# Attention scores of two heads at a time on the two 64-row halves of the TensorE array

## The chip, the cores and the metric

The kernel runs on one core of a Trainium2 chip. The time is device microseconds (us) of one execution. A profiled execution also leaves a trace with the start, the length and the waits of each instruction on each engine: PE is TensorE's matrix products, PEld its loads of stationary weights, DVE VectorE, ACT ScalarE, POOL GpSimd, SP the engine that issues most weight transfers.

## The reference

Two transformer layers on one sequence of 512 tokens and 1024 channels, in float32, each with adaptive norms (`ada_w` times an activated vector gives shifts, scales and gates), an attention and a mixture of 32 experts.

```python
def diff_attention(h, ...):                 # layer 0: 8 heads, two maps (cc) of 64 channels each
    q, k, v = split(h @ w_in, 3)            # rotary on the first 16 of each 64 channels
    s = einsum('cbhqd,cbhkd->cbhqk', qb, k) * d ** -0.5      # d = 64, causal
    a = softmax(s[0]) - lam_full * softmax(s[1])
    o = rmsnorm(a @ v) ...
def nsa_attention(h, ...):                  # layer 1: 16 heads of 64 channels, 2 kv groups
    s_c = qb . k_cmp     # 31 compressed blocks; p_c @ v_cmp
    s_s = qb . k_sel     # all 8 blocks are selected: plain causal attention, own k and v
    s_w = qb . k_win     # window of 512: plain causal attention, own k and v
    o = g0 * o_c + g1 * o_s + g2 * o_w
x = x + g1 * attention(...);  x = x + g2 * hier_moe(...)
```

## The kernel before

Products that need more than one fast pass are split by hand: a float32 tensor is written as a high part in `F32R` (a float32 type that one pass of the array takes) and the rest, a low part, and three products (high.high, high.low, low.high) are added up in PSUM. `dense` does this for the projections: for each of 8 chunks of the contraction it makes `wh` (ACT, L346) and `wl` (DVE, L347) and runs three products for each of four token tiles (L350 to L352).

A head has 64 channels and the array has 128 rows, and the kernel fills the other 64 rows with the split. The query and key rows that come out of a projection are copied twice side by side (`twice`, `dup_in`: L492, L493 in layer 0, L1044 in layer 1), rotated by `rope` on POOL (four instructions, L305 to L308), and transposed 128 columns at a time (L500, L1051), so that each head's 64 channels stand in rows 0 to 63 and again in rows 64 to 127. `stack_q` (L362 on ACT, L363 on DVE) then makes one tile with the high part of q in rows 0 to 63 and the low part in rows 64 to 127. `stack_k` (L358, L359) makes two tiles of k, high and low, each of them in both halves. In `scores`, one product of the stacked q with high k gives high.high plus low.high (L367), one with low k gives the rest (L369), and between them an identity in bf16 adds the causal mask to the last 128 columns (L368). The result of one head for 128 queries and n keys (n is 128, 256, 384 or 512, for query tile i = 0 to 3) fills n columns of one PSUM bank.

`softmax_rows` takes the row maximum on DVE (L374) and the exponential with its sum on ACT (L375) from that bank. There are eight banks, in three kinds: "mm" (4, also the accumulators of `dense` and of the adaptive norms, L189), "sc" (2) and "tr" (2, for transposes). Layer 0 takes its scores in "sc" alone; layer 1 takes "sc" twice and "mm" three times in every five heads.

The work of layer 0 is written out in an order (`v0 h0 q1 a8 h1 h2 ...`: v and q units are projections, h are heads, a are steps of the adaptive norms); `diff_rows` (one head, one query tile: two `scores`, softmaxes, difference, transposes L535, product with v L540) has a higher priority than what is around it, and a scheduler at build time places each engine's instructions by its own simulation. Layer 1 runs `nsa_block(gi, i)` for two kv groups and four query tiles: for "s" and "w", eight heads of scores in two batches of four, a scaling (L1189), then for each key tile eight transposes (L1197), two copies (L1199) and two products with v (L1202). The compressed scores are done in the "w" half: 16 products of 32 columns (L1149, L1150) in one bank.

The experts follow each attention: 16 pairs of experts a layer, whose two halves stand in columns 0 to 63 and 64 to 127 of the array (`pair`, L852). Their weights are 100.7 MB a layer, fetched by SP into tiles (`slot0` to `slot7`, `ring`) that the attention uses too, as these come free.

## Time and profile before

| | |
|---|---|
| median of 3 runs | 1419.81 us (1417.21 to 1421.36) |
| the profiled execution | 1417.2 us, its span in the trace 1415.4 us |
| mean granted TensorE clock | 0.957 of full speed |
| PE busy | 1289.2 us, 91% of the span |
| DVE, ACT, POOL busy | 787.2, 513.0, 188.4 us |

The span goes from the first to the last instruction; 1.8 us of the execution lie around it. Matrix products overlap in the array, and the trace models their ends, so a length of 0.40 us does not say that the array was taken for so long: the time from one start to the next says that, and it is what is read below. Layer 0's projections and heads stand at about 60 to 320 us, its experts at about 390 to 660, layer 1's projections at 700 to 815, its attention blocks at 815 to 1045, its experts from about 1130 on.

### The profile page before, as it was taken

The page shows a single profiled execution, that of the slowest core. Times are in us where ns is not written, and L with a number is a line of the kernel's source. Part 1 is how long each engine was busy: PE and PEld are TensorE (multiplying, and loading weights), DVE is VectorE, ACT ScalarE, POOL GpSimd, SP SyncE. Part 2 cuts the span into 40 slices and gives each one's busy share as a digit, 9 for nine tenths or more (in the row PEclk, how much of TensorE's full clock was granted, in tenths as well). Part 3 has the DMA queues.
Part 4 walks back from the last instruction along what each step waited for, and adds up shares of the span by engine and source line. Part 5 has one row for each costly group of instructions (what it writes and reads, how often), then busy time and mean ns, then how long its engine had stood idle before and what let it go on. Part 6 is the DMA issues. An engine that isn't in the chain of part 4 may idle for free.

```text
span 1415.4 us, 18254 instructions
## 1 busy us (share of the span) xinstructions
PE 1289.2 (91%) x6431; PEld 760.4 (54%) x6431; DVE 787.2 (56%) x1791; ACT 513.0 (36%) x1188; POOL 188.4 (13%) x298
## 2 busy tenths in 40 slices
PE   4899999978879999999799799999999599999995
PEld 0687658567733544444588465556558434444342
DVE  2444756486535666655653365657635445666555
ACT  2453544454322222111453345555644222222212
POOL 0022020211110000000042211112120200000000
PEclk7999999989979999999899999999999799999998
DMA  8633673585569999992132474520063599999931
GB/s 265 218 92 129 226 236 122 185 280 194 181 240 362 389 408 407 380 346 95 52 110 90 126 251 138 139 70 1 30 183 119 167 363 376 401 409 408 363 144 60
DMA packets 104494, 309.82 MB, mean 219 GB/s; under 512 B 13776, under 2 KB 27568, under 8 KB 104388
## 3 DMA queue, kind: packets, MB, share of 16 engines
q1 hardware_dynamic: 93920, 288.59, 57.4%
q0 software_dynamic: 6240, 12.95, 2.7%
q10 hardware_dynamic: 4228, 6.96, 1.6%
q8 instruction: 55, 0.90, 0.3%
q14 instruction: 51, 0.42, 0.1%
HBM read 310.51 MB, written 6.33 MB: 224 GB/s over the span
## 4 chain that ended last, share of the span: by engine, by line
PE 65%; DVE 6%; DMA 3%; ACT 2%; issue 1%; POOL 1%; DVEq 0%; POOLq 0%; ACTq 0%
PE b_mm L852 17%; PE b_mm L1202 5%; PE b_sc L875 4%; PE b_mm L875 4%; PE b_tr L1197 3%; PE b_sc L886 2%; PE b_tr L840 2%; PE b_mm L886 2%; DVE xs L888 2%; PE b_mm L350 2%; PE b_mm L572 2%; PE b_mm L573 2%; PE b_mm L351 2%; PE b_mm L352 2%; PE b_mm L574 2%; PE b_sc L887 2%
## 5 line engine op out<-in xcount | busy, mean ns | idle before, releaser
L852 PE MATMUL b_mm<-slot,xT 128*64 128x512 f32 x640 | 200.0, 607 | 0.0
L852 PE MATMUL b_mm<-ring,xT 128*64 128x512 f32 x384 | 135.9, 597 | 0.0
L350 PE MATMUL b_mm<-wh,h_hi 128*128 128x512 f32 (+1 forms) x320 | 116.6, 394 | 8.3 <-ACT wh L346 6.6
L351 PE MATMUL b_mm<-wl,h_hi 128*128 128x512 f32 (+1 forms) x320 | 122.1, 390 | 0.0
L352 PE MATMUL b_mm<-wh,h_lo 128*128 128x512 f32 (+1 forms) x320 | 119.9, 386 | 0.0
L845 ACT ACTIVATE xT<-b_tr,col_sh,col_A 128x128 f32<-128x128 f32 x128 | 56.4, 454 | 148.2 <-DVE xT L847 146.9
L852 PEld LDWEIGHTS b_mm<-slot,xT 128*64 128x64 f32 x640 | 58.3, 139 | 87.7 <-issue 81.7
L888 DVE TENSOR_TENSOR xs<-xs,b_sc 128x512 f32<-128x512 f32 x128 | 83.1, 680 | 23.1 <-PE b_sc L887 23.1
L888 DVE TENSOR_TENSOR xs<-xs,b_mm 128x512 f32<-128x512 f32 x128 | 81.9, 679 | 19.3 <-PE b_mm L887 19.3
L826 POOL DMA_INDIRECT xg<-xr_d,toks x32 | 32.1, 1003 | 434.1 <-PE b_tr L840 417.5
L189 PE MATMUL b_mm<-ring,csil 128*32 128x512 f32 x384 | 79.2, 645 | 10.5 <-DMA ring<-in_ada_w_dram 5.6
L855 ACT ACTIVATE sl<-b_mm 128x256 f32<-128x256 f32 x32 | 12.3, 384 | 187.7 <-PE b_mm L852 187.7
L857 DVE TENSOR_TENSOR ac<-b_mm,sl 128x256 f32<-128x256 f32 x32 | 19.8, 618 | 108.4 <-ACT sl L855 108.4
L347 DVE TENSOR_TENSOR wl<-ring,wh 128x512 fp32r<-128x512 f32 (+1 forms) x80 | 53.6, 679 | 38.3 <-ACT wh L346 37.6
L374 DVE TENSOR_REDUCE nm<-b_sc 128x1 f32<-128x128 f32 (+3 forms) x116 | 54.4, 482 | 32.2 <-PE b_sc L369 31.2
L350 PEld LDWEIGHTS b_mm<-wh,h_hi 128*128 128x128 f32 x320 | 60.5, 192 | 20.1 <-ACT wh L346 7.5
L1199 ACT ACTIVATE pT<-b_tr 128x512 f32<-128x512 f32 x80 | 47.3, 597 | 62.6 <-PE b_tr L1197 62.2
L358 ACT ACTIVATE yh<-y 128x512 fp32r<-128x512 f32 x64 | 39.9, 632 | 79.4 <-DVE y L878 79.4
L352 PEld LDWEIGHTS b_mm<-wh,h_lo 128*128 128x128 f32 x320 | 60.7, 190 | 11.0
L351 PEld LDWEIGHTS b_mm<-wl,h_hi 128*128 128x128 f32 x320 | 60.6, 190 | 10.9
L852 PEld LDWEIGHTS b_mm<-ring,xT 128*64 128x64 f32 x384 | 39.9, 137 | 49.4 <-issue 46.7
L346 ACT ACTIVATE wh<-ring 128x512 fp32r<-128x512 f32 (+1 forms) x80 | 48.4, 614 | 46.3 <-PE b_mm L352 38.0
(327 smaller groups left out, 2683.5 us busy)
## 6 DMA issues: line engine op xcount, KB each, us to landing
ring<-in_ada_w_dram SPq DMA_DIRECT2D x96, 512.0 KB
slot<-in_moe_w_gate_dram SPq DMA_DIRECT2D x80, 512.0 KB
slot<-in_moe_w_up_dram SPq DMA_DIRECT2D x80, 512.0 KB
dn<-in_moe_w_down_dram SPq DMA_DIRECT2D x80, 512.0 KB
slot<-in_moe_w_down_dram SPq DMA_DIRECT2D x48, 512.0 KB
ring<-in_moe_w_gate_dram SPq DMA_DIRECT2D x48, 512.0 KB
ring<-in_moe_w_up_dram SPq DMA_DIRECT2D x48, 512.0 KB
ring<-in_diff_w_in_dram SPq DMA_DIRECT2D x24, 512.0 KB
```

The costliest lines, as they stand in the source:

```text
L189: mm(acc[32 * g:32 * g + 32, :], lhsT, w[:, c0:c0 + 512], start=(k == 0), stop=(k == KC - 1), skip_group_check=True)
L347: nc.vector.tensor_tensor(wl[:, :n], w[:, k, :], wh[:, :n].bitcast(F32), op=OP.subtract)
L350: mm(accs[t][:, :n], hi[:, k, tt], wh[:, :n], start=(k == 0), stop=False)
L351: mm(accs[t][:, :n], hi[:, k, tt], wl[:, :n], start=False, stop=False)
L352: mm(accs[t][:, :n], lo[:, k, tt], wh[:, :n], start=False, stop=(k == KC - 1))
L374: nc.vector.tensor_reduce(nm, b[:, :n], axis=AX.X, op=OP.max, negate=True)
L845: nc.scalar.activation(xT[:, k, :], src, AF.Identity, scale=g.Ac[:, k:k + 1], bias=g.shc[:, k:k + 1])
L852: mm(hb[64 * a:64 * a + 64, :].rearrange("p (z n) -> p z n", z=2), xT[:, k, 64 * a:64 * a + 64], gu(a, k), start=(k == 0), stop=(k == KC - ...
L875: mm(yb[64 * a:64 * a + 64, :], aT[:, k, 64 * a:64 * a + 64], dn(a, k, z), start=(k == 0), stop=(k == 1), skip_group_check=True)
L886: mm(b, st[:, t * P:(t + 1) * P], yh[:, zz], start=True, stop=False)
L888: nc.vector.tensor_tensor(g.xs[:, t, zz], g.xs[:, t, zz], b, op=OP.add)
L1202: mm(ob[64 * st:64 * st + 64, :], vst[nm][:, j, 64 * gi:64 * gi + 64], pTs[st], start=(nm == "s" and j == 0), stop=False, skip_group_check ...
```

## The change

Heads 2s and 2s+1 now stand side by side: rows 0 to 63 of a tile hold the 64 channels of the one, rows 64 to 127 those of the other, without any copy. So `rope` takes 8 blocks of 64 and not 16, a token tile needs four transposes and not eight, and one `stack_k` over q and k together (layer 0) or over q (layer 1) takes the place of two calls. `scores` takes two heads and two banks: each product exists twice, once on rows 0 to 63 and once on rows 64 to 127, written alternately, and the three parts high.high, high.low and low.high are now three products of 64 rows a head. The mask, whose contraction runs over 128 positions, is added in two halves of 64 a head (`id2`, `mask2`). In layer 0 both maps of a head are one such pair, with both "sc" banks; in layer 1 the two heads of a pair share k, whose tiles already hold it in both halves. The compressed scores become 24 products on 64 rows, in two banks, with two additions of the mask.

```diff
--- before.py
+++ after.py
@@ -141,10 +141,16 @@
     nc.gpsimd.iota(jp, pattern=[[1, P]], base=0, channel_multiplier=-1, allow_small_or_imprecise_dtypes=True)
     ident = cst.tile([P, P], F32, name="ident")
     nc.vector.tensor_scalar(ident, jp, 0.0, None, op0=OP.is_equal)
-    ident_b = cst.tile([P, P], BF16, name="ident_b")
-    nc.vector.tensor_scalar(ident_b, jp, 0.0, None, op0=OP.is_equal)
-    maskneg = cst.tile([P, P], BF16, name="maskneg")
-    nc.vector.tensor_scalar(maskneg, jp, 0.0, NEG, op0=OP.is_gt, op1=OP.mult)
+
+    j2 = ring[1][:, P:2 * P]
+    for a in range(2):
+        nc.gpsimd.iota(j2[64 * a:64 * a + 64], pattern=[[1, P]], base=0, channel_multiplier=-1,
+                       allow_small_or_imprecise_dtypes=True)
+    id2 = cst.tile([P, 2, P], BF16, name="id2")
+    mask2 = cst.tile([P, 2, P], BF16, name="mask2")
+    for z in range(2):
+        nc.vector.tensor_scalar(id2[:, z], j2, 64.0 * z, None, op0=OP.is_equal)
+        nc.vector.tensor_scalar(mask2[:, z], j2, 64.0 * z, NEG, op0=OP.is_gt, op1=OP.mult)
     upper = cst.tile([P, P], BF16, name="upper")
     nc.vector.tensor_scalar(upper, jp, 0.0, None, op0=OP.is_gt)
     ones_b = cst.tile([P, P], BF16, name="ones_b")
@@ -358,16 +364,20 @@
         nc.scalar.activation(h_out, src, AF.Copy)
         nc.vector.tensor_tensor(l_out, src, h_out.bitcast(F32), op=OP.subtract)
 
-    def stack_q(src, dst):
-        nc.scalar.activation(dst, src, AF.Copy)
-        nc.vector.tensor_tensor(dst[64:128], src[64:128], dst[64:128].bitcast(F32), op=OP.subtract)
-
-    def scores(q, kh, kl, n, i, tag="sc"):
-        b = bank(tag)
-        mm(b[:, :n], q, kh, start=True, stop=False)
-        mm(b[:, i * P:n], ident_b, maskneg, start=False, stop=False, skip_group_check=True)
-        mm(b[:, :n], q, kl, start=False, stop=True)
-        return b
+    def scores(qh, ql, kh, kl, n, i, tags):
+
+        bs = [bank(tag) for tag in tags]
+        rows = [slice(0, 64), slice(64, 128)]
+        for a, b in enumerate(bs):
+            mm(b[:, :n], qh[rows[a]], kh[rows[a]], start=True, stop=False)
+        for z in range(2):
+            for a, b in enumerate(bs):
+                mm(b[:, i * P:n], id2[rows[a], z], mask2[rows[a], z], start=False, stop=False, skip_group_check=True)
+        for a, b in enumerate(bs):
+            mm(b[:, :n], qh[rows[a]], kl[rows[a]], start=False, stop=False)
+        for a, b in enumerate(bs):
+            mm(b[:, :n], ql[rows[a]], kh[rows[a]], start=False, stop=True)
+        return bs
 
     def softmax_rows(b, n, p_out, l_out):
         nm = sm.tile([P, 1], F32, name="nm")
@@ -484,26 +494,20 @@
         w = unit().rearrange("p (k n) -> p k n", k=KC)
         wload(w[:, :, 0:256], w_in[:, :, u * 256:(u + 1) * 256])
         wload(w[:, :, 256:512], w_in[:, :, D + u * 256:D + (u + 1) * 256])
-        qs, kh, kl = (slot(2 * i + u % 2, [P, 4, S], F32R) for i in range(3))
-        ST[u] = (qs, kh, kl)
+        qkh, qkl = (slot(2 * i + u % 2, [P, 4, S], F32R) for i in range(2))
+        ST[u] = (qkh, qkl)
 
         def evac(t, acc):
-            tmp = m.tile([P, 16, 64], F32, name="qkt", bufs=2)
-            nc.scalar.activation(twice(tmp[:, 0:8, :]), dup_in(acc[:, 0:256], 64), AF.Copy, scale=0.125)
-            nc.scalar.activation(twice(tmp[:, 8:16, :]), dup_in(acc[:, 256:512], 64), AF.Copy)
-            rope(m, tmp, t, 16)
+            tmp = m.tile([P, 8, 64], F32, name="qkt", bufs=2)
+            nc.scalar.activation(tmp[:, 0:4, :], acc[:, 0:256].rearrange("p (s d) -> p s d", d=64), AF.Copy, scale=0.125)
+            nc.scalar.activation(tmp[:, 4:8, :], acc[:, 256:512].rearrange("p (s d) -> p s d", d=64), AF.Copy)
+            rope(m, tmp, t, 8)
+            b = bank("tr")
+            for s in range(4):
+                nc.tensor.transpose(b[:, s * P:(s + 1) * P], tmp[:, 2 * s:2 * s + 2, :].rearrange("p a d -> p (a d)"),
+                                    ident)
             tt = slice(t * P, (t + 1) * P)
-            for half in range(2):
-                b = bank("tr")
-                for s in range(4):
-                    c0 = 2 * (half * 4 + s)
-                    nc.tensor.transpose(b[:, s * P:(s + 1) * P], tmp[:, c0:c0 + 2, :].rearrange("p a d -> p (a d)"),
-                                        ident)
-                bv = b.rearrange("p (s t) -> p s t", s=4)
-                if half == 0:
-                    stack_q(bv, qs[:, :, tt])
-                else:
-                    stack_k(bv, kh[:, :, tt], kl[:, :, tt])
+            stack_k(b.rearrange("p (s t) -> p s t", s=4), qkh[:, :, tt], qkl[:, :, tt])
 
         dense(qp, w, 512, hi, lo, evac, before)
 
@@ -515,14 +519,14 @@
         V[u] = v
         dense(qp, w, 512, hi, lo, lambda t, acc: copy_any(v[:, t, :], acc))
 
-    def diff_rows(h, i, qs, kh, kl, v, hc):
+    def diff_rows(h, i, qkh, qkl, v, hc):
         n = (i + 1) * P
         es = m.tile([P, 2, 512], F32, name="es", bufs=2)
         l2 = sm.tile([P, 2], F32, name="l2")
+        s = h % 2
+        bs = scores(qkh[:, s, i * P:n], qkl[:, s, i * P:n], qkh[:, 2 + s, :n], qkl[:, 2 + s, :n], n, i, ("sc", "sc"))
         for cc in range(2):
-            s = 2 * (h % 2) + cc
-            b = scores(qs[:, s, i * P:n], kh[:, s, :n], kl[:, s, :n], n, i)
-            softmax_rows(b, n, es[:, cc, :n], l2[:, cc:cc + 1])
+            softmax_rows(bs[cc], n, es[:, cc, :n], l2[:, cc:cc + 1])
 
         r = sm.tile([P, 2], F32, name="r2")
         nc.vector.tensor_scalar(l2, l2, 1e-30, None, op0=OP.max)
@@ -543,12 +547,12 @@
         nc.vector.tensor_scalar(o_n[:, i, h * P:(h + 1) * P], ob[:, 0:P], r[:, 0:1], None, op0=OP.mult)
 
     def diff_head(h):
-        qs, kh, kl = ST[h // 2]
+        qkh, qkl = ST[h // 2]
         v = V[h // 4]
         hc = slice((h % 4) * P, (h % 4 + 1) * P)
         for i in range(NT):
             with tc.high_priority(offset=0):
-                diff_rows(h, i, qs, kh, kl, v, hc)
+                diff_rows(h, i, qkh, qkl, v, hc)
         r = rsqrt_cols(oss[:, h, :], NT, 1.0 / P)
         for i in range(NT):
             oo = o_n[:, i, h * P:(h + 1) * P]
@@ -1041,16 +1045,14 @@
 
         def evac(t, acc):
             tmp = tp.tile([P, 16, 64], F32, name="qkt", bufs=4)
-            nc.scalar.activation(twice(tmp), dup_in(acc, 64), AF.Copy, scale=0.125)
-            rope(m, tmp, t, 16)
+            q8 = tmp[:, 0:8, :]
+            nc.scalar.activation(q8, acc.rearrange("p (s d) -> p s d", d=64), AF.Copy, scale=0.125)
+            rope(m, q8, t, 8)
             tt = slice(t * P, (t + 1) * P)
-            for half in range(2):
-                b = bank("tr")
-                for s in range(4):
-                    c0 = 2 * (half * 4 + s)
-                    nc.tensor.transpose(b[:, s * P:(s + 1) * P], tmp[:, c0:c0 + 2, :].rearrange("p a d -> p (a d)"),
-                                        ident)
-                stack_q(b.rearrange("p (s t) -> p s t", s=4), qs[half][:, :, tt])
+            b = bank("tr")
+            for s in range(4):
+                nc.tensor.transpose(b[:, s * P:(s + 1) * P], q8[:, 2 * s:2 * s + 2, :].rearrange("p a d -> p (a d)"), ident)
+            stack_k(b.rearrange("p (s t) -> p s t", s=4), qs[0][:, :, tt], qs[1][:, :, tt])
 
         dense(qp, w, 512, hi, lo, evac)
 
@@ -1144,12 +1146,18 @@
         for zi, nm in ((1, "s"), (2, "w")):
             if nm == "w":
 
-                b = bank("sc")
-                for h in range(8):
-                    mm(b[:, 32 * h:32 * h + 32], qs[h // 4][:, h % 4, tt], kch[:, 32 * gi:32 * gi + 32], start=True, stop=False)
-                    mm(b[:, 32 * h:32 * h + 32], qs[h // 4][:, h % 4, tt], kcl[:, 32 * gi:32 * gi + 32], start=False, stop=True)
+                bs = [bank("sc") for _ in range(2)]
+                rows = [slice(0, 64), slice(64, 128)]
+                gg = slice(32 * gi, 32 * gi + 32)
+                for s in range(4):
+                    for x, (qq, kk) in enumerate(((0, kch), (0, kcl), (1, kch))):
+                        for a in range(2):
+                            mm(bs[a][:, 32 * s:32 * s + 32], qs[qq][rows[a], s, tt], kk[rows[a], gg], start=(x == 0),
+                               stop=(x == 2))
                 sc = m.tile([P, 8, 32], F32, name="scm", bufs=2)
-                nc.vector.tensor_tensor(sc, b[:, 0:256].rearrange("p (h n) -> p h n", h=8), dup(mcmp[:, i, :], 8), op=OP.add)
+                for a in range(2):
+                    nc.vector.tensor_tensor(sc[:, a:8:2, :], bs[a][:, 0:P].rearrange("p (h n) -> p h n", h=4),
+                                            dup(mcmp[:, i, :], 4), op=OP.add)
                 mx = sm.tile([P, 8], F32, name="cmx")
                 nc.vector.tensor_reduce(mx, sc, axis=AX.X, op=OP.max)
                 nc.vector.tensor_tensor(sc, sc, mx[:, :, None].to_broadcast([P, 8, 32]), op=OP.subtract)
@@ -1174,12 +1182,15 @@
                     Pt = (m if pt[0] % 4 == 2 else m1).tile([P, 4, S], F32, name="Pt", tag="P", bufs=1)
                 Ps.append(Pt)
                 l4 = sm.tile([P, 4], F32, name="l4")
-                for hh in range(4):
-                    h = 4 * st + hh
-                    bb = scores(qs[h // 4][:, h % 4, tt], kst[nm][gi][0][:, 0:n], kst[nm][gi][1][:, 0:n], n, i,
-                                "mm" if sct[0] % 5 > 1 else "sc")
-                    sct[0] += 1
-                    softmax_rows(bb, n, Pt[:, hh, 0:n], l4[:, hh:hh + 1])
+                for s in range(2 * st, 2 * st + 2):
+                    tags = []
+                    for _ in range(2):
+                        tags.append("mm" if sct[0] % 5 > 1 else "sc")
+                        sct[0] += 1
+                    bs = scores(qs[0][:, s, tt], qs[1][:, s, tt], kst[nm][gi][0][:, 0:n], kst[nm][gi][1][:, 0:n], n, i, tags)
+                    for a in range(2):
+                        hh = 2 * (s % 2) + a
+                        softmax_rows(bs[a], n, Pt[:, hh, 0:n], l4[:, hh:hh + 1])
                 r = sm.tile([P, 4], F32, name="r4")
                 nc.vector.tensor_scalar(r, l4, 1e-30, None, op0=OP.max)
                 nc.vector.reciprocal(r, r)
```

## Rows read from the trace of the kernel before

**Rows 1.** The page: engines; the chain that ended last, by engine.

```profile
PE 1289.2 (91%) x6431; PEld 760.4 (54%) x6431; DVE 787.2 (56%) x1791; ACT 513.0 (36%) x1188; POOL 188.4 (13%) x298
...
PE 65%; DVE 6%; DMA 3%; ACT 2%; issue 1%; POOL 1%; DVEq 0%; POOLq 0%; ACTq 0%
```

**Rows 2.** Busy us (x instructions) in four stretches, granted clock, DMA.

```profile
60.00:280.00 220.00, 216.99 (x1157) 155.16 (x1156) 119.40 (x278) 101.11 (x257) 42.48 (x69) 1.00 0.50 161
280.00:320.00 40.00, 31.52 (x173) 24.32 (x172) 31.97 (x98) 22.19 (x75) 4.41 (x5) 0.87 0.88 283
...
780.00:815.00 35.00, 24.31 (x126) 15.86 (x126) 13.73 (x27) 10.60 (x19) 10.34 (x16) 0.93 0.42 128
815.00:1045.00 230.00, 228.77 (x1251) 124.97 (x1252) 135.79 (x405) 124.61 (x353) 38.43 (x32) 0.99 0.35 109
```

**Rows 3.** PE in time order: heads of 512 columns; start, length.

```profile
1001.93 0.40 PE L367 MATMUL b_mm<-slot,slot 128*128 128x512 f32 x1
1002.18 0.23 PE L368 MATMUL b_mm<-maskneg,ident_b 128*128 128x128 bf16 x1
1002.22 0.47 PE L369 MATMUL b_mm<-slot,slot 128*128 128x512 f32 x1
1002.53 0.40 PE L367 MATMUL b_mm<-slot,slot 128*128 128x512 f32 x1
...
1002.81 0.47 PE L369 MATMUL b_mm<-slot,slot 128*128 128x512 f32 x1
1003.21 1.07 PE L1202 MATMUL b_mm<-pT,v_w 128*64 128x512 f32 x2
```

**Rows 4.** PE in time order: heads of 128 and of 256 columns.

```profile
950.18 0.27 PE L367 MATMUL b_mm<-slot,slot 128*128 128x128 f32 x1
...
950.48 0.27 PE L367 MATMUL b_mm<-slot,slot 128*128 128x128 f32 x1
...
952.40 0.28 PE L367 MATMUL b_mm<-slot,slot 128*128 128x256 f32 x1
...
952.76 0.28 PE L367 MATMUL b_mm<-slot,slot 128*128 128x256 f32 x1
```

**Rows 5.** PE in time order: heads of 384 columns.

```profile
971.57 0.34 PE L367 MATMUL b_mm<-slot,slot 128*128 128x384 f32 x1
...
972.05 0.34 PE L367 MATMUL b_mm<-slot,slot 128*128 128x384 f32 x1
```

**Rows 6.** PE in time order: two products of a projection, 512 columns.

```profile
222.53 0.39 PE L350 MATMUL b_mm<-wh,h_hi 128*128 128x512 f32 x1
222.76 0.39 PE L351 MATMUL b_mm<-wl,h_hi 128*128 128x512 f32 x1
```

**Rows 7.** PE in time order: first and last of 16 compressed scores.

```profile
1004.21 0.28 PE L1149 MATMUL b_sc<-kch,slot 128*128 128x32 f32 x1
...
1005.91 0.26 PE L1150 MATMUL b_sc<-kcl,slot 128*128 128x32 f32 x1
```

**Rows 8.** Weight loads in time order: start of an expert pair.

```profile
423.96 0.13 PEld L852 LDWEIGHTS b_mm<-slot,xT 128*64 128x64 f32 x1 [0.25 <-issue]
423.96 0.13 PEld L852 LDWEIGHTS b_mm<-ring,xT 128*64 128x64 f32 x1
424.01 0.14 PEld L852 LDWEIGHTS b_mm<-slot,xT 128*64 128x64 f32 x1
```

**Rows 9.** PE in time order: an expert pair, and what follows.

```profile
549.24 6.60 PE L852 MATMUL b_mm<-ring,xT 128*64 128x512 f32 x29
555.77 0.51 PE L886 MATMUL b_sc<-yh,st 128*128 128x512 f32 x1
```

**Rows 10.** PE in time order: transposes of one token tile.

```profile
780.51 1.03 PE L1051 MATMUL b_tr<-ident,qkt 128*128 128x128 f32 x8
```

**Rows 11.** Groups by line: transposes, row maximum.

```profile
L500 PE MATMUL b_tr<-ident,qkt 128*128 128x128 f32 x128 | 19.3, 280 | 1.1 <-DVE slot L363 1.1
...
L374 DVE TENSOR_REDUCE nm<-b_sc 128x1 f32<-128x512 f32 x28 | 18.8, 685 | 8.2 <-PE b_sc L369 8.1
```

## The prediction

> **What bounds the kernel now.** I read the page first, then the busy time by stretches, then PE in order of time. The page says that PE is busy for 91% of the span and that 65% of the chain that ended last runs through it, DVE next with 6% [rows 1]. The stretches say where that matters for this change. From 60 to 280 us (projections and heads 0 to 5 of layer 0) PE is busy 217 of 220 us, from 815 to 1045 us (the blocks of layer 1) 228.8 of 230, at a granted clock of 1.00 and 0.99 of full speed, while DVE, ACT and DMA are near half or under [rows 2]. There a microsecond less on PE should be a microsecond less of time. Two stretches are otherwise: 280 to 320 us, where the last heads have little beside them (PE 31.5 of 40, DVE 32.0), and 780 to 815 us, the end of layer 1's projections (PE 24.3 of 35) [rows 2]. The experts take what comes before them as a starting line: their weights are loaded into tiles that the attention has to leave, so that an earlier end of the attention moves them forward whole.
>
> What a head costs on PE is read from start to start. Four heads of 512 columns in a row: high product to mask 0.25, mask to low product 0.04, low product to the next head 0.31 us; 0.60 in all [rows 3]. With 384 columns a head takes 0.48, with 256 0.36, with 128 0.30 [rows 4, 5]. There are 192 heads, 48 of each size: 48 x 1.74 = 83.5 us of PE when nothing stands between them, and somewhat more as they lie, since a run of heads that ends on a product of another shape costs 0.40 at its end and not 0.31 (low product at 1002.81, L1202 at 1003.21) [rows 3].
>
> **What two halves of the array do together.** No product of before uses 64 rows, so this is the price that the trace does not hold. The nearest rows are products on 64 columns. One alone (L1202, two passes) takes from 1003.21 to 1004.21, 0.50 a pass [rows 3, 7]. An expert pair alternates between the two column halves, and 29 passes of the same length take 6.53 us, 0.225 each [rows 9]: two halves run side by side. Their weight loads too: the first loads of the two halves start within 0.01 us of each other, and the second load of the first half follows 0.05 later [rows 8], so that each half has a queue of its own. I take the same for row halves: the two heads of a pair cost what one costs. The bounds are that, and no overlap at all.
>
> The Trainium skill ("TensorE: Matmul & The Clock Gate", Part 3, Measured speedup vs the span model) gives 3.07 for four row tiles of 32 at 512 columns; as an estimate from that figure, three quarters of full overlap would put the pairs at 2.53 + 0.63 = 3.16, and the scores' term at -7.7 in place of -22.8. No run here shows it yet.
>
> **The change part by part.** *Scores.* A head on its half now has high product, two masks, low product and a third product. That is the old head plus one mask (0.04) plus one product. A product with its load hidden costs 0.23 at 512 columns [rows 6], and I take three quarters of that, 0.17, at 384. At 256 and 128 columns the load of the weights sets the pace: in the compressed scores, whose products have only 32 columns, the 16th product starts 1.70 after the first [rows 7], 15 steps of 0.113, so I take 0.12 and 0.11. New heads: 0.87, 0.69, 0.52, 0.45, sum 2.53 for a pair of each size against 2 x 1.74 = 3.48. Side by side that is 0.95 less for each four pairs, and there are 24 such fours: **-22.8 us**. With no overlap the same sum is 2 x 2.53 = 5.06, 1.58 more, +37.9 us.
>
> *Change of shape.* A pair that stands between products of 128 rows changes the array's shape twice. The row for such a step is the 0.40 against 0.31 above: 0.09 [rows 3]. 96 calls, in layer 1 two behind each other: about 64 runs x 2 x 0.09 = 11.5 us if each is new, nothing if each run stands between expert-like shapes as the one in [rows 3] does, which pays it already. I take **+4 us**, nearer to the second, since L1202 and L189 (both on part of the columns) are the commonest neighbours. The Trainium skill ("TensorEngine Tiling (Array Packing)", Key Properties) says against the change that a new tiling mode drains the engine; the trace agrees, with 0.09 us a step, and by the rule alone each of the 128 steps would be new, 7 us more than I take.
>
> *Compressed scores.* 16 loads become 24, on two queues 12: 12 x 0.113 = 1.36 against 1.81, eight blocks, **-3.6 us**; in one queue 2.71, +7.2 us. The second addition on DVE (off the path: DVE is at 136 of 230 us [rows 2]) costs nothing here.
>
> *Transposes.* Eight a token tile take 1.03 us with the last one's length of 0.27 to 0.28 in it, 0.108 each [rows 10, 11]. Layer 0 has 128 of them [rows 11], layer 1 64 by the code; half go: 96 x 0.108 = **-10.4 us**.
>
> *ACT, DVE, POOL, DMA.* Half of the copies, one of two splits and half of `rope` go in 24 token tiles; the constants gain a few instructions in the first 60 us, before the first head. All of it lies beside PE: in 60 to 280 us DVE is at 119, ACT at 101, POOL at 42 of 220 [rows 2]. Without that cover (780 to 815 us) a token tile's chain is shorter by about one split; I count that as part of the next allowance. No transfer is added or moved; the weights of the experts still wait for the same tiles.
>
> *Both banks at once.* In layer 0 a pair fills both "sc" banks, so the next pair waits for two softmaxes and not for one. A row maximum of 512 columns takes 0.69 [rows 11], the exponential behind it about the same. Where projections run beside the heads that is hidden; from 280 to 320 us it is not. Ten calls there at 0.7 would be +7 us, nothing where DVE is the slower anyway (32.0 of 40 us [rows 2]). In layer 1 the small query tiles (128 and 256 columns) may find ACT, at 125 of 230 us, no longer covered. For all of this I keep back 5 of the gain.
>
> Sum: -22.8 + 4 - 3.6 - 10.4 = -32.8, and 5 kept back, **-28 us**. The profiled execution took 1417.2 us, which is the lowest of the times shown but for one hundredth; the median is 1419.8. From 1417.2 the sum gives 1389; from the median 1392. I say **1390 us**.
>
> **The rivals.**
>
> 1. *The row halves do not overlap.* For it: no product of before shows it, and both halves read the same queue of instructions. Against it: the column halves do overlap, products and loads [rows 8, 9]. Scores +37.9, compressed +7.2, transposes -10.4, shape +4: about +39 us, 1456. This is the way to the other side. It decides from about half of full overlap: 24 fours may cost 3.48 + (10.4 - 4) / 24 = 3.75 before the gain of the transposes is gone, and between 5.06 (none) and 2.53 (full) that is 52%.
> 2. *Products overlap, weight loads do not.* Then six loads at 0.113 and four of the masks at 0.04 are a floor of 0.84 for a pair; 512 columns take 0.87 plus one late load, 0.98. Sum 3 x 0.84 + 0.98 = 3.50 against 3.48: nothing won in the scores, +7.2 in the compressed ones, -10.4, +4: about +1 us, 1418 to 1421. Against it the loads in [rows 8]; those are of column halves.
> 3. *The softmax takes the gain.* Overlap is there, but PE waits for banks: half of the scores' gain and 7 us more at 280 to 320 are lost, about -14 us, 1404. For it: pairs need two banks at once. Against it: ACT and DVE are idle for nearly half of 815 to 1045 [rows 2].
>
> **How the numbers follow.** The forecast 0.58 (its own range 1376 to 1400: all of the 33 and some of the shorter chains at one end, half of it at the other), rival 1 0.17, rival 2 0.13, rival 3 0.12. A measurement of this kernel can tell about 0.3%, 4 us. Faster: 0.58 + 0.12 + 0.04 of rival 2 = 0.74; the same 0.06; slower 0.17 + 0.03 = 0.20. The range leaves out rival 1 and a little at the low end: 1370 to 1432, which also holds half of an overlap with all its changes of shape.
>
> **What the profile after would show.** In a run of paired heads of 512 columns the two products of a pair start within some 0.02 us of each other and a pair lasts about 0.87 us; 1.7 us would be rival 1. The loads of the two halves start together; if they stand 0.11 apart, it is rival 2. 815 to 1045 us gets shorter by some 18 us, 60 to 320 by 10 to 14, the experts by nothing. If PE shows new waits for ACT's exponential (L375) in front of the first products, it is rival 3. The forecast is wrong if 64-row products on two banks take turns, if the scheduler puts other products between those of a pair, or if the clock, now 1.00 in these stretches, falls with half of the rows in use.

## The result and the profile after

| | before | after |
|---|---|---|
| median of the runs, us | 1420.59 (1417.21 to 1425.71) | 1444.38 (1440.57 to 1446.62) |
| ratio | 1 | 1.0168, 95% interval 1.0147 to 1.0190 |
| span of the profiled execution, us | 1415.4 | 1443.1 |
| last product with v of layer 0's heads, us from the start | 315.1 | 317.8 |
| first expert product of layer 0 | 401.0 | 405.1 |
| last product of layer 1's projections | 780.3 | 784.4 |
| start of layer 1's blocks | 812.1 | 811.7 |
| last product with v in the blocks | 1044.8 | 1073.0 |

The change makes the kernel slower by 23.8 us; 1390 was forecast. The last five lines of the table are starts in PE's records, of one profiled execution each. Almost all of the loss lies in layer 1's blocks, 261 us in place of 233. Layer 0, where ten to fourteen us should have been won, is 3 us late.

The first line below is the page's for PE, the others are busy time by stretches (PE, PEld, DVE, ACT, POOL, then granted clock, DMA share, GB/s), three of the stretches of [rows 2], of the kernel after.

```profile
PE 1321.9 (92%) x6783; PEld 773.5 (54%) x6783; DVE 775.6 (54%) x1777; ACT 492.9 (34%) x1164; POOL 171.3 (12%) x300
...
60.00:280.00 220.00, 220.00 (x1193) 152.11 (x1191) 107.28 (x264) 88.03 (x245) 29.28 (x69) 1.00 0.50 163
280.00:320.00 40.00, 35.74 (x188) 26.65 (x187) 29.74 (x91) 19.71 (x68) 4.43 (x5) 0.79 0.79 263
...
815.00:1045.00 230.00, 228.23 (x1438) 128.84 (x1438) 132.16 (x393) 112.56 (x326) 36.33 (x30) 0.94 0.29 92
```

PE is as full as before, by 33 us more in all, and DVE, ACT and POOL have less to do than in [rows 1, 2]. So the loss is more time on PE, not a wait for another engine. The granted clock of 815 to 1045 us went from 0.99 to 0.94.

PE in order of time shows what a pair costs. The first lines are one of the few pairs whose two heads alternate as written (x2 and x4 are products of both halves), the lines after "..." a place where one head of 512 columns stands by itself.

```profile
107.98 0.50 PE L372 MATMUL b_sc<-slot 64*128 64x512 f32 x2
108.32 0.29 PE L375 MATMUL b_sc<-mask,id 64*128 64x128 bf16 x4
108.42 0.48 PE L377 MATMUL b_sc<-slot,slot 64*128 64x512 f32 x2
108.73 0.40 PE L379 MATMUL b_sc<-slot,slot 64*128 64x512 f32 x2
109.06 0.50 PE L356 MATMUL b_mm<-wh,h_hi 128*128 128x512 f32 x1
...
142.40 0.50 PE L372 MATMUL b_sc<-slot 64*128 64x512 f32 x1
142.75 0.28 PE L375 MATMUL b_sc<-mask,id 64*128 64x128 bf16 x2
142.84 0.47 PE L377 MATMUL b_sc<-slot,slot 64*128 64x512 f32 x1
143.16 0.39 PE L379 MATMUL b_sc<-slot,slot 64*128 64x512 f32 x1
143.48 0.62 PE L195 MATMUL b_mm<-ring,csil 128*32 128x512 f32 x2
```

From 107.98 to 109.06, two heads take 1.08 us; from 142.40 to 143.48, one head takes 1.08 us too. So the halves do run side by side, loads included, and rivals 1 and 2 are out as they were put: the second head is free. But the first lines are the exception. By the order of their starts, the ten products of a pair stand in the written order, with no other score beside them, 8 times. The five of one head stand alone 38 times, and most other pairs are staggered, the second head some products behind the first, since the scheduler places each product when its own simulation finds it ready. And 1.08 us, for two heads or one, is not the 0.87 that was forecast.

To see where the PE time went I summed PE's records from start to start, by kind of product, over layer 1's blocks (from the start of the first to the last product with v, idle time apart), and counted how often one product has another shape of the array (rows by columns) than the one ahead of it:

| blocks of layer 1, us | before | after | pinned | batch_runs | mask_64 |
|---|---|---|---|---|---|
| length | 233.2 | 261.5 | 241.8 | 254.6 | 261.3 |
| scores of the heads | 66.6 | 70.1 | 57.5 | 56.1 | 94.1 |
| compressed scores | 14.4 | 20.3 | 12.9 | 12.8 | 14.3 |
| transposes of the probabilities | 38.7 | 48.3 | 46.6 | 47.7 | 38.2 |
| products with v, both kinds | 86.2 | 89.6 | 87.1 | 89.9 | 87.2 |
| steps of the adaptive norms, rest | 25.4 | 30.3 | 30.6 | 28.0 | 26.5 |
| PE idle | 1.7 | 2.6 | 7.2 | 20.0 | 0.8 |
| changes of shape | 176 | 260 | 244 | 231 | 425 |

Between before and after every kind grew, the untouched transposes of the probabilities by as much as any: +9.6 us for the same 320 instructions. Over the whole kernel changes of shape went from 429 to 582. The other columns are experiments.

### The profile page after: what moved, and what is told of

Its sections match the earlier page's. It is cut to its first block, busy times and chain, and to the rows that moved or that the text cites. A ratio compares the mean times of both kernels' runs of the same rounds, so it can differ in the third digit from the quotient of the medians.

```text
span 1443.1 us, 18884 instructions
## 1 busy us (share of the span) xinstructions
PE 1321.9 (92%) x6783; PEld 773.5 (54%) x6783; DVE 775.6 (54%) x1777; ACT 492.9 (34%) x1164; POOL 171.3 (12%) x300
## 3 DMA queue, kind: packets, MB, share of 16 engines
q1 hardware_dynamic: 93920, 288.59, 55.9%
## 5 line engine op out<-in xcount | busy, mean ns | idle before, releaser
L358 PEld LDWEIGHTS b_mm<-wh,h_lo 128*128 128x128 f32 x320 | 60.6, 189 | 11.3 <-issue 0.4
```

What stands on the lines that cost most here:

```text
L358: mm(accs[t][:, :n], lo[:, k, tt], wh[:, :n], start=False, stop=(k == KC - 1))
```

## The experiments

Two theories at first. *Order*: the pairs would give what was forecast if their products stood together. *Shapes*: each run of 64-row products costs a change of the array's shape on the way in and out, however it is ordered. A third, *banks*, came with layer 0's end.

**pinned.** The ten products of a pair, and the 24 compressed scores of a block, are tied in their written order for the scheduler; nothing else.

```diff
+    def in_order(start):
+        chain = [i for i in nc.cur_bb.bb.instructions[start:] if i.engine == mybir.EngineType.PE]
+        for x, y in zip(chain, chain[1:]):
+            tc.add_manual_dep(y, x.name, ...NoSync...)
...
         bs = [bank(tag) for tag in tags]
+        at = traced_now()
...
+        in_order(at)
         return bs
```

> The changed kernel with the ten products of a pair, and the 24 compressed scores of a block, tied in the order in which they are written (first half, second half, first half, ...); nothing else. Theory 'order': the two row halves overlap in the array, but the scheduler had put one head's five products behind each other, so that the overlap was seldom used. In the trace of the changed kernel a pair whose products alternate takes 1.08, 0.91, 0.73 and 0.61 us for 512, 384, 256 and 128 columns, and a head alone takes the same. With all 96 pairs alternating the scores go from 118 to 24 x 3.3 = 80 us of PE and the compressed scores from 20 to 12: 1444 falls by 30 to 46 us, to 1398 to 1414 us. Rival 'array': the halves take turns in the array whatever the order: 1440 to 1448. Rival 'work': third product, second mask and changes of shape cost the 24 us by themselves: 1430 to 1444.

1431.11 us, ratio to before 1.0074 (1.0057 to 1.0091). That misses the range of theory *order* and lies at the low end of rival *work*'s. The order is worth 13 us, and the kernel is still 11 us slower than before. In layer 1's blocks the scores now take 57.5 us against 66.6 before and the compressed ones 12.9 against 14.4, so the pairs do give PE time back; it goes to the transposes of the probabilities (+7.9), the remaining kinds (+6.1) and idle PE (+5.5).

**apart.** The ten products of a pair are tied as in pinned, but the five of one half stand ahead of the five of the other; the compressed scores are left to the scheduler again.

```diff
-        for z in range(2):
-            for a, b in enumerate(bs):
-                mm(... mask ...)
+        for a, b in enumerate(bs):
+            mm(... high.high ...); two masks; mm(... high.low ...); mm(... low.high ...)
```

> The changed kernel with the five products of one head tied behind each other and both heads no longer alternating as written; nothing else. Theory 'order': the third or so of the heads that still ran side by side lose it, 20 to 30 pairs at about 0.7 us: 1450 to 1465 us. Rival 'array': no difference, 1440 to 1448.

1447.65 us (1.0200, 1.0179 to 1.0220): about what the kernel after takes, 1444. By the ranges alone this speaks for rival *array*; what rules that rival out is pinned, and the two heads in 1.08 us above. The change as it stood was timed with most of its pairs undone. Apart is 16.5 us over pinned, of which some 6 are the compressed scores, which take 18.8 us here and 12.9 in pinned. A pair of 512 columns in this order, and the product behind it:

```profile
245.49 0.50 PE L383 MATMUL b_sc<-slot 64*128 64x512 f32 x1
...
245.84 0.49 PE L383 MATMUL b_sc<-slot 64*128 64x512 f32 x1
...
246.91 0.38 PE L553 MATMUL b_tr<-slot,aT 128*128 128x128 f32 x1
```

The second head starts 0.35 us behind the first and runs beside its later products: 1.42 us for both, between the 1.08 of alternating products and the 2.16 of two heads alone. So the halves overlap fully where their products alternate in PE's order, and in part where one five follows the other.

**layer0_alone, layer1_alone.** The change in one layer only, without ties.

```text
layer0_alone:  q_unit, nsa_block of layer 1 as before
layer1_alone:  qk_unit, diff_rows of layer 0 as before
```

> The change in layer 0 alone; layer 1 as before (copies, stacked q, two products a head). In the two traces the last product of layer 0's heads comes 2.7 us later with the change and layer 1's blocks take 28.6 us longer. All theories that place the loss in layer 1's blocks expect 1419 to 1426 us. If layer 0 costs more than its own end shows (through the experts' weights), it is over 1430.

> The change in layer 1 alone; layer 0 as before. If the loss lies in layer 1's blocks, 1438 to 1446 us; if it comes from layer 0, 1418 to 1425.

1430.46 (1.0078, 1.0061 to 1.0095) and 1436.14 us (1.0114, 1.0095 to 1.0132): +10.6 and +16.3, together 27 where both cost 24. Each layer loses by itself; layer 1 alone comes out 2 us under the range that puts the whole loss there. A look at the table of stages alone would have put it all on layer 1. Layer 0's code is the same in layer0_alone and in the kernel after, and PE's order there all but the same, yet its last product with v starts at 321.7 us in the one profile and at 317.8 in the other, with a granted clock of 0.65 and 0.79 from 280 to 320 us. So a difference of 4 us at the end of layer 0 between two single profiles can be the clock alone.

**mask_64.** The kernel before, with the mask's product on 64 rows in place of 128 (the mask of the lower 64 query rows is left out).

```diff
-        mm(b[:, i * P:n], ident_b, maskneg, start=False, stop=False, skip_group_check=True)
+        mm(b[:, i * P:n], ident_b[0:64], maskneg[0:64], start=False, stop=False, skip_group_check=True)
```

> The kernel before with one edit: the mask's product of every head works on 64 of the 128 array rows instead of all (it leaves out the mask of the lower 64 query rows). As many products, columns and loads as before; only the array's shape changes twice more in each of 192 heads. Theory 'changes of shape': in the traces so far a product in front of another shape lasts some 0.09 us longer and the first product behind it some 0.06 us longer, so 384 changes at 0.10 to 0.15 give 38 to 58 us, 1458 to 1478 us. Theory 'order' (the halves were taken apart, and a change as such is all but hidden): within 6 us of before, 1414 to 1426.

1470.72 us, 1.0355 (1.0291 to 1.0418). The number of instructions, columns and loads is that of before; 385 more changes of shape cost 51.8 us, **0.135 us each** in the mean (the interval of the ratio, 41 to 59 us, makes it 0.11 to 0.15). Not all of that is the change itself: behind layer 0's projections, where the clock is at its lower level from 297 to 338 us, 48 more changes go with 11 us. In layer 1's blocks, by the table, 249 more changes add 27.5 us to the scores, 0.11 each. PE in order of time, heads of 512 columns of this kernel, to be held against [rows 3]:

```profile
1054.75 0.40 PE L367 MATMUL b_mm<-slot,slot 128*128 128x512 f32 x1
1055.08 0.23 PE L368 MATMUL b_mm<-maskneg,ident_b 64*128 64x128 bf16 x1
1055.23 0.50 PE L369 MATMUL b_mm<-slot,slot 128*128 128x512 f32 x1
1055.57 0.40 PE L367 MATMUL b_mm<-slot,slot 128*128 128x512 f32 x1
```

High product to mask 0.33 in place of 0.25, mask to low product 0.15 in place of 0.04, low product to the next head 0.34 in place of 0.31: 0.82 a head and not 0.60, 0.11 for each of two changes. So a change is paid on both sides of it: the product ahead of it lasts 0.08 longer, and the one behind it starts late by its load. In the kernel before, the loads of L369 and of the next head's L367 start at 1002.18 and 1002.30, ahead of their products at 1002.22 and 1002.53 [rows 3]; behind the change above, load and product start together at 1055.23. The loads, of the kernel before and then of mask_64:

```profile
1002.18 0.20 PEld L369 LDWEIGHTS b_mm<-slot,slot 128*128 128x128 f32 x1
1002.30 0.19 PEld L367 LDWEIGHTS b_mm<-slot,slot 128*128 128x128 f32 x1
```

```profile
1055.23 0.19 PEld L369 LDWEIGHTS b_mm<-slot,slot 128*128 128x128 f32 x1
```

The same two signs stand in the paired kernels. First PE in the kernel before, a head behind four transposes of the probabilities, then the same place in both_banks (below), a pair of 256 columns behind four transposes; in both a product with v or another shape stands ahead of the transposes.

```profile
894.45 0.65 PE L1197 MATMUL b_tr<-ident,Pt 128*128 128x128 f32 x4
894.86 0.48 PE L367 MATMUL b_sc<-slot,slot 128*128 128x512 f32 x1
```

```profile
840.30 0.66 PE L1231 MATMUL b_tr<-ident,Pt 128*128 128x128 f32 x4
840.89 0.38 PE L385 MATMUL b_sc<-slot,slot 64*128 64x256 f32 x1
```

Four transposes take 0.41 us in front of a 128-row head and 0.59 in front of a pair: 0.18 for the way in, booked on the transposes. In the kernel after, 49 of these runs of transposes stand in front of a 64-row product, and none did before: 49 x 0.18 = 8.8 of their +9.6 us. The next rows are two pairs of 512 columns behind each other, in pinned.

```profile
927.41 0.50 PE L383 MATMUL b_sc<-slot,slot 64*128 64x512 f32 x1
...
927.75 0.23 PE L386 MATMUL b_sc<-mask,id 64*128 64x128 bf16 x1
...
928.16 0.39 PE L390 MATMUL b_sc<-slot,slot 64*128 64x512 f32 x1
...
928.39 0.40 PE L383 MATMUL b_mm<-slot,slot 64*128 64x512 f32 x2
928.63 0.28 PE L386 MATMUL b_mm<-mask,id 64*128 64x128 bf16 x4
928.72 0.48 PE L388 MATMUL b_mm<-slot,slot 64*128 64x512 f32 x2
929.04 0.40 PE L390 MATMUL b_mm<-slot,slot 64*128 64x512 f32 x2
929.36 1.07 PE L1227 MATMUL b_mm<-pT,v_s 128*64 128x512 f32 x2
```

High product to mask takes 0.34 in the first pair and 0.24 in the second; the last product lasts 0.23 when a pair follows and 0.32 when another shape does. A pair with a pair on either side is 0.24 + 0.09 + 0.32 + 0.23 = 0.88: the forecast 0.87. A pair alone is 1.08.

**both_banks.** In pinned, 17 first products still went out alone, with other work behind them, because their bank was free and the second half's was not. Here the first product also waits for the exponential that frees the second "sc" bank.

```diff
+        first = [i for i in nc.cur_bb.bb.instructions[at:] if i.engine == mybir.EngineType.PE][0]
+        if tags[1] in read_by:
+            tc.add_manual_dep(first, read_by[tags[1]], ...Sync...)
```

> The kernel 'pinned' with one more edge: the first product of a pair also waits for the exponential that frees the second of the two 'sc' banks, so that a first product no longer goes out alone with other work behind it. On paper 110 runs of score products in place of 121, in layer 0 nearly all ten products long. Theory 'changes of shape', at about 0.35 us for each run (in, out, and the neighbours): 4 us less than pinned's 1431, 1425 to 1429. Theory 'banks' (a pair waits for two softmaxes): the later start costs more than it gives, 1433 to 1440.

1429.61 us (1.0066, 1.0045 to 1.0087): no difference from pinned that can be measured. The profile shows two things that cancel. The last product of layer 0's projections starts at 250.3 us, 10 earlier than in pinned and 9 earlier than in the kernel before; there the pairs and the halved transposes pay. But what follows to the last product with v takes 67.4 us against 55.9 before, with PE idle for 15.6 against 8.6. Busy time in this kernel, the same columns as above:

```profile
280.00:290.00 10.00, 5.75 (x34) 4.37 (x34) 8.09 (x25) 4.70 (x18) 1.02 (x1) 0.67 0.88 294
290.00:300.00 10.00, 8.68 (x47) 6.27 (x47) 6.08 (x19) 3.89 (x15) 0.00 (x0) 0.50 0.77 262
300.00:310.00 10.00, 8.10 (x44) 5.32 (x42) 7.41 (x25) 3.92 (x16) 1.01 (x1) 0.67 0.01 4
```

PE's waits here end with work of the last heads on DVE and ACT (transposed rows, exponentials), and the clock granted to it falls to 0.67 and 0.50, which is the lower level of 1.2 GHz for much or all of the time; PE was busy for 6.5 of the 10 us from 270 to 280, in which it first falls. While the clock is low, what PE still has to do runs at half speed.

**batch_runs.** As both_banks, and in layer 1 the two pairs of a batch of four heads are one run of twenty products.

```diff
+                for s, tag in ((2 * st, "sc"), (2 * st + 1, "mm")):
+                    bs += scores(..., (tag, tag))
+                in_order(at)
+                for hh in range(4):
+                    softmax_rows(bs[hh], n, Pt[:, hh, 0:n], l4[:, hh:hh + 1])
```

> The kernel 'both_banks', and in layer 1 the twenty products of a batch of four heads are tied into one run, the first pair on the two 'sc' banks and the second on two 'mm' banks. On paper 98 runs in place of pinned's 121. Theory 'changes of shape': 23 runs less at 0.35 us and the second pair of a run at 0.87 in place of 1.08 us for 512 columns: 8 to 16 us under pinned's 1431, 1415 to 1423. Theory 'banks': four exponentials have to end before the next batch begins, PE waits in layer 1's blocks, 1433 to 1450.

1437.86 us (1.0121, 1.0100 to 1.0143): 8 us more than both_banks where 8 to 16 less than pinned were expected. A miss for *shapes* taken alone; the time is in the range of *banks*. In the table above there are 13 changes fewer than in pinned, the scores give back 1.4 us, and PE idles for 20.0 us instead of 7.2. But the wait that grew isn't the one that *banks* names. Two of PE's waits in the blocks, from 812.5 us to the last product with v (us in total, times, longest), of batch_runs and then of both_banks:

```profile
PE b_mm L1234 <- ACT pT L1231: 11.3, 8, 5.2
PE b_sc L385 <- ACT slot L403: 2.5, 3, 1.0
```

```profile
PE b_mm L1236 <- ACT pT L1233: 0.5, 2, 0.3
PE b_mm L385 <- ACT slot L403: 2.8, 5, 1.2
```

The scores wait for exponentials no longer than they did; the products with v wait 11.3 us for ACT's copies of the transposed probabilities. Probably ACT has the four exponentials of a batch ahead of these copies; that was not tested by itself.

**banks_tail.** As pinned, and the last two heads of layer 0 use "sc" and "mm" banks in turn.

```diff
-..., n, i, ("sc", "sc"))
+..., n, i, ("mm", "mm") if h > 5 and i % 2 else ("sc", "sc"))
```

> The kernel 'pinned' with one edit: the pairs of the last two heads of layer 0 use the 'sc' and the 'mm' banks in turn, so that a pair there doesn't wait for the softmaxes of the pair ahead of it. Theory 'banks': the stretch from the last projection to the last head of layer 0, 63 us in pinned and 56 in the kernel before, gets its 7 us back, 1423 to 1426. Theory 'changes of shape and the clock that falls there': no difference that can be measured, 1428 to 1434.

1432.56 us (1.0092, 1.0072 to 1.0112), pinned's time. Its profiled execution was the fastest of the four, 1427.4, and there the stretch behind the projections took 56.9 us as *banks* has it; the other three took 1432 to 1434, so that profile doesn't speak for them. Left open by this run.

**layer0_pairs, layer0_best.** Layer 0 as in both_banks, layer 1 as in the kernel before; the second also with banks_tail's edit.

> Layer 0 as in 'both_banks' (pairs of ten products in one run, the first waiting for both banks), layer 1 as in the kernel before: 35 runs of 64-row products in all. In both_banks the projections of layer 0 ended at 249 us, 9 us ahead of the kernel before, and the last two heads behind them took 68 us in place of 56, with 16 us of idle PE and 38 us at half clock. Theory 'changes of shape' for layer 1: without its 70 or so runs the time comes down from 1430 by the 11 us that layer 1's blocks lost, 1417 to 1421. Theory that layer 1's loss is the end of layer 0 that comes later: it stays at 1426 to 1431.

> The kernel 'layer0_pairs', and the pairs of the last two heads of layer 0 use the 'sc' and the 'mm' banks in turn. Theory 'banks' for the stretch behind layer 0's projections: the wait for both softmaxes goes, the stretch takes 57 us as in 'banks_tail', and the 9 us won beside the projections stay, 1407 to 1413. Theory 'softmax chain and clock': the last heads are as long as their chain through ACT and DVE wherever the banks are, PE idles and its clock falls there, 1416 to 1421.

1425.47 (1.0039, 1.0025 to 1.0053) and 1421.59 us (1.0008, 0.9994 to 1.0022). The first is between both theories: layer 1's blocks are back at 232 us, but layer 0 ends at 319.8, 5 us after the kernel before, and what comes behind it, experts included, moves with it. The second is the best paired kernel, and no faster than before. The 32 exponentials of its last two heads take from 282.0 to 302.6 us (280.9 to 311.5 in both_banks, 283.4 to 308.7 before), so the second pair of banks does shorten the end. Still, the 7 us by which the last product of its projections starts earlier, at 251.7, shrink to 2 at the last product with v, 313.0: PE idles for 12.7 us there, with the clock between 0.60 and 0.75 from 280 to 310. From there to the first expert product it takes 88.4 us against 85.9, so that the experts start at 401.4 where they started at 401.0. The time is that of *softmax chain and clock*, but not all of its mechanism: the exponentials do end 6 us earlier than before, and what takes the gain back comes behind them, with PE's clock low. How much of that is the clock wasn't separated.

**half_transposes.** The other half of the change alone: q and k copied once, four transposes for eight; then ACT and DVE build the stacked tiles of the kernel before, crossing from one half of the partitions to the other.

```diff
+    def stack_q(src, dst):
+        for a, own, other in halves():
+            nc.scalar.activation(dst[own, a::2], src[own], AF.Copy)
+            nc.vector.tensor_tensor(dst[other, a::2], src[own], dst[own, a::2].bitcast(F32), op=OP.subtract)
```

> The transposes' half of the change alone: each token tile's q and k are copied once and transposed in four blocks in place of eight, and the stacked tiles of the kernel before are filled from them by ACT and DVE, from 64 array rows' worth of partitions to the other 64 where needed; scores as before, on all 128 rows. More and shorter copies on ACT and DVE, 96 transposes less on PE, not one change of shape more. Theory 'the transposes' term stands, and what ate it are the changes of shape': 10.4 us less on PE, of which the stretches where PE is the bound give most back, 1407 to 1413. Theory 'PE's saved microseconds are lost to copies, banks or the clock whatever the scores do': 1416 to 1424.

1423.60 us (1.0027, 1.0011 to 1.0042). A miss: halving the transposes in this way wins nothing. On PE the gain is all there (the transposes of layer 0's q and k take 8.1 us for 14.7, and the last product of its projections starts at 253.8, 5.3 earlier), without one change of shape more. Then comes this, in its busy time by stretches:

```profile
270.00:280.00 10.00, 4.58 (x24) 2.11 (x22) 9.04 (x24) 4.95 (x13) 0.00 (x0) 0.79 0.90 302
280.00:290.00 10.00, 5.00 (x19) 3.85 (x19) 7.66 (x20) 6.38 (x21) 1.36 (x2) 0.50 0.89 290
```

DVE, busy for 9.04 of 10 us, has the splits of the last token tiles besides the softmaxes; PE is busy for 4.58, and in the next 10 us its clock is at the lower level. The first two of PE's waits from 270 to 316 us (us in total, times, longest):

```profile
PE b_tr L542 <- DVE slot L374: 4.5, 1, 4.5
PE b_tr L509 <- DVE slot L374: 2.9, 1, 2.9
```

PE waits 7.4 us for low parts of q and k, which this edit cut into more pieces: layer 0 has 96 such splits on DVE and not 32, and the last one starts at 285.6 us, where the last of the kernel before started at 283.2. Layer 0's last product with v starts at 316.5, 1.4 after the kernel before. In that kernel PE was busy for 31.5 of 40 us from 280 to 320, and DVE for 32.0 [rows 2]: the end of layer 0 is a chain through DVE, ACT and PE, and here DVE holds its start where it was. So this run doesn't say what the halved transposes would be worth without the extra splits, as in the kernel after, where one split a token tile is left.

**two_products.** As both_banks, without the third product of each head (low q times high k is left out).

```diff
-            mm(b[:, :n], qh[rows[a]], kl[rows[a]], start=False, stop=False)
-        for a, b in enumerate(bs):
-            mm(b[:, :n], ql[rows[a]], kh[rows[a]], start=False, stop=True)
+            mm(b[:, :n], qh[rows[a]], kl[rows[a]], start=False, stop=True)
```

> The kernel 'both_banks' without the third product of each head (it leaves out the low part of q times the high part of k). By the steps of pinned's runs that product takes 0.31, 0.26, 0.20 and 0.14 us for a pair of 512, 384, 256 and 128 columns, 0.91 for four pairs, 22 us for 24 fours. Theory 'PE sets the time, also where the pairs are': 1406 to 1412. Theory 'softmax and banks set it': 1420 to 1428.

1415.71 us, 0.9975 of before (0.9956 to 0.9995), with runs from 1410.6 to 1425.8. By the medians 14 us less than both_banks, by the profiled executions 20 (spans 1408.8 and 1428.9): between the two theories, nearer to PE. Layer 1's blocks go from 245 to 232 us, 13 of the 14.6 that the estimate gives for their 16 fours (16 x 0.91): there PE's time is nearly all the kernel's time, also in the paired version, so that what pairs cost in changes of shape should be paid there in much the same measure.

## Why the prediction was wrong

*Two halves at once: right.* A pair whose products alternate takes what one head takes, 1.08 us. Rivals 1 and 2 don't describe the array. What came nearest to rival 1's end, a time above before, came another way.

*"The two heads of a pair cost what one costs", for every pair: failed in the order.* The price holds for products that alternate in PE's order, and I took the written order for the issued one. That the scheduler might put other products between was named as what would make the forecast wrong, and given no price and no chance. pinned puts it at 13 us of the kernel's time.

*"New heads: 0.87, 0.69, 0.52, 0.45": right inside a run, wrong as the pairs lie.* A pair between pairs takes 0.88. A pair alone, and most are alone, takes 1.08, 0.91, 0.73 and 0.61 for the four sizes, 3.33 and not 2.53. The 3.48 for two old heads of each was the price inside a run as well: as they lay, the old heads took 101.5 / 24 = 4.2. The scores' term, even with all pairs together, was -5 over both layers by the sums from start to start (101.5 us before, 96.5 in pinned), and -11 in both_banks (90.2); -22.8 was forecast, and +14 (115.5) came. In layer 1's blocks pinned wins 9.1 us in the scores and loses 14 on the products beside them.

*"Change of shape: +4" is the step that decided.* The row it came from, 0.40 against 0.31, is the way out of a head into another shape, which the kernel before paid already. I took its 0.09 as the price of any change and then most changes as paid by the neighbours. But the kernel before has 128-row scores next to 128-row transposes, four at a time, and no change between them; these are the places where each pair now gets one on either side. I counted 64 runs of paired products; there are 130 runs of 64-row products, those of the compressed scores among them. There are 153 changes more; at mask_64's 0.11 to 0.135 us they come to 17 to 21 us. In the rows above a change costs the product ahead of it some 0.09, four transposes 0.18, and the product behind it the load that it can no longer hide; the first of these is booked on instructions that nobody touched. The Trainium skill ("TensorEngine Tiling (Array Packing)", Key Properties) says that a change of tiling mode drains the engine. The traces agree, with 0.11 to 0.135 us each here. The prediction cited it and then sided with the cheaper reading of one row.

*Compressed scores: -3.6 forecast, +5.9 came.* The rule of the two queues was right and again lost to the order: in most of the eight blocks the scheduler issues the products of one half and then those of the other. PE of the kernel after, in order of time:

```profile
846.59 0.28 PE L1155 MATMUL b_sc<-kch,slot 64*128 64x32 f32 x1 [0.45 <-ACT Pt L385]
846.72 0.26 PE L1155 MATMUL b_sc<-kcl,slot 64*128 64x32 f32 x1
846.83 0.37 PE L1155 MATMUL b_sc<-kch,slot 64*128 64x32 f32 x2
```

Each takes 0.11 to 0.13 us, with nothing beside it: 24 of them at full clock are the 2.7 us of the bound without overlap, and the mean of the eight blocks is 2.5. In pinned, all 24 in one run take 1.44 and 1.48 us (two blocks), against the 1.36 of the forecast, and the eight blocks 12.9, -1.5.

*Transposes: -10.4 forecast, -10.0 on PE (22.6 to 12.6 us), and no time that a run shows from it.* The term was counted as time because PE is busy for nearly all of 60 to 280 us. It is, and the projections did end earlier; but the last heads behind them don't follow. Their end was seen in [rows 2] and given 5 us of allowance; 5 of the 7 us that layer0_best has won by the end of the projections are lost there, and all 5 of half_transposes, whose extra splits on DVE are part of it. Rival 3 had this mechanism, with 7 us for it; there it stood beside a gain in layer 1 that didn't come.

*The clock.* It was named as a risk. In the kernel after, the granted clock is at its lower level for some 7 us more than before in 280 to 320 (17.1 us against 10.2 by the trace's clock records; mean 0.79 against 0.87) and for some 20 us more in 815 to 1045 (26.0 against 5.5; mean 0.94 against 0.99). Of the second, some 10 us of full-speed work are lost, part of the growth in the table. Which products bring it down wasn't separated from the rest: two of the falls, at 848 and at 998 us, come 1 and 3 us after the start of compressed scores on one half at a time, with PE busy for 7.55 of the 8 us from 840 and for all 8 from 990, and in pinned, where those are short, the stretch is back at 0.97.

What stays open: how the 24 us divide between order (13 by pinned), changes of shape (17 to 21 by the price of mask_64), the clock, and the gains against them, since each was taken with the others present; and what the halved transposes are worth in time.

## What to carry to other kernels

Before packing small products into parts of the array, count how often the array's shape will change in the order in which PE gets its instructions, neighbours included, and price each change from a run of its own; packing pays where many packed products stand behind each other. Side by side is a property of the issued order: tie the partners together, or the build's scheduler may take them apart, as it did here. And a gain on the busiest engine is only a gain up to the next stretch that another chain sets; look first where that stretch begins and whether its start would move.

## What the runs showed of the hardware that was not expected

- A change between products on 128 rows and products on 64 rows costs 0.11 us where it is read from start to start in a head (0.82 against 0.60 us for two), and 0.135 us in the mean of 385 over the whole kernel (51.8 us, 41 to 59). It is seen on both sides: four transposes ahead of it take 0.59 us and not 0.41, and the step of the first product behind it is 0.34 and not 0.24.
- 64-row products on the two halves that alternate in PE's order overlap fully, weight loads included, at 128 to 512 columns (1.08 us for the ten products of two heads of 512 columns, 1.08 for the five of one). Five behind five overlap in part (1.42 us in apart).
- At the end of layer 0 both_banks was granted less clock than the kernel before (0.50 to 0.67 against 0.73 to 0.93 from 280 to 310 us) while PE waited more there (15.6 us against 8.6). That the waits brought the clock down isn't shown: the kernel after waited less there than the one before (4.2 us idle behind its projections) and had a lower clock too (0.79 against 0.87 from 280 to 320).
